# A two-layer decoder trunk on one core: in the attention phases the low halves of the weights, the reciprocals, scalings and copies are emitted some tiles later, and the scores and outputs stand at other tiles

## The chip, the core and the metric

The kernel runs on one core of a Trainium2 chip. The core has a matrix engine (PE, with its weight loads shown as PEld), a vector engine (DVE), a scalar engine (ACT), GpSimd (POOL) and a queue engine that issues the transfers (SP). Each engine runs its own instructions in the order in which the program emitted them and waits for the others by semaphores. The metric is the device time of one execution in microseconds (us); the kernel before takes 544.97 us (median of 3 runs, 544.86 to 545.21).

## The reference, cut to what matters

```
x: 256 tokens x 1024, one sequence; 2 layers; mod = silu(c) @ w_mod[i] + b_mod[i]
layer 0 mixer: causal pooling; layer 1 mixer: attention; after each mixer a squared-ReLU MLP
def moba_attention(h, w_qkv, w_o, rel_bias):      # 16 heads of 64; one block of 256 keys
    q, k, v = split(h @ w_qkv)
    logits = q @ k.T * 64**-0.5 + bias[bucket(distance)]; masked above the diagonal
    o = softmax(logits) @ v
    return o @ w_o
x = x + gate * mixer(modulate(rmsnorm(x)))
x = x + gate * (relu(h @ w_up) ** 2 @ w_down)     # w_up 1024 x 4096, w_down 4096 x 1024
```

All is float32. A block of 256 keys covers the whole sequence, so the choice of blocks drops out.

## The kernel before

Activations lie transposed (128 channels by 256 tokens). Every weight matrix is cut in 128 x 128 tiles, and all tiles of all matrices stand in one stream in the order in which PE uses them; eight tiles are a step. A transfer (`issue`, five 1 MB buffers) brings two steps. For precision each step is split in two: ACT rounds it to a high part `w_hi` (L256), DVE subtracts to get the low part `w_lo` (L266), both three steps ahead of their use. A tile is then two or three matmuls (L278, L279 where the high part meets high and low activations in one 512-column matmul; L284 to L286 otherwise). PE is fed by these streams nearly without a gap; everything else is laid beside them.

The order of all this is written out by hand. `next_columns` is called once for each tile and counts tiles in `now`. `later(d, fn)` puts a piece of work into the program `d` tiles later, `at(t, fn)` puts it at tile `t` of the attention phase. At each multiple of eight it also emits the split of a later step and, at some steps, half of a late modulation vector (`mod_dve`, L308: a product of 128 x 1024 on DVE with a sum along the row). What is emitted earlier stands earlier in its engine's queue; times follow from that and from the waits.

The attention phase counts tiles from 0: tiles 0 to 63 make q and k of head pairs 0 to 3, 64 to 95 the values of these pairs, 96 to 159 q and k of pairs 4 to 7, 160 to 191 their values, 192 to 255 the product with w_o. For each of eight head pairs `p` the class `Pair` emits: `done` (q and k from PSUM to `qk`; for pairs 4 to 7 a copy on ACT, L1021, and an addition on DVE, L1022), `scores` at tile `SCORES_AT[p]` (eight matmuls `sc`, L1031), then with `later` the logits and their row maxima on DVE (L1047, L1053), the exponentials on ACT (L1059), the reciprocals of the sums on DVE (L1064), the scalings on ACT (L1070), the transposes on PE (`pt`, L1076), their copies on ACT (`PT`, L1078), and `outputs` at tile `OUTPUTS_AT[p]` (eight matmuls `po`, L1088 and L1089), split on ACT and DVE into `ol` (L1093, L1096). `qkv_normed` makes the normalised input in eight pieces, with two products on GpSimd (L997, L998) and the two parts on ACT (L494) and DVE (L497).

Of the kernel before, what the change touches and what calls it, by code (L numbers as in the profile page):

```python
# [8 lines left out]
F32 = mybir.dt.float32  # L9
F32R = mybir.dt.float32r  # L10
AF = mybir.ActivationFunctionType
# [4 lines left out]
P = 128  # L16
S = 256
# [62 lines left out]
STEP_QKV = STEP_DN0 + DN_STEPS  # L80
STEP_WO = STEP_QKV + QKV_STEPS
STEP_UP1 = STEP_WO + WO_STEPS
STEP_DN1 = STEP_UP1 + UP_STEPS
# [19 lines left out]
AHEAD = 3  # L103
# [4 lines left out]
N_NORMED, NORMED_AT, NORMED_GAP = 16, 30, 11  # L108

QKV_NORMED_AT, QKV_NORMED_GAP = 29, 6  # L110
SCORES_AT = (46, 65, 84, 103, 122, 138, 155, 172)
OUTPUTS_AT = (108, 116, 125, 145, 203, 208, 213, 218)

# [32 lines left out]
def tile_hybrid_pool_moba(  # L148
# [12 lines left out]
    nc = tc.nc  # L161
# [6 lines left out]
    tmp = ctx.enter_context(tc.tile_pool(name="tmp", bufs=2))  # L168
# [4 lines left out]
    def bank(name):  # L173
        return ps.tile([P, 512], F32, tag="ps", name=name)

    def al_tile(shape, name, dt=F32):
        return act.tile(shape, dt, tag="al", bufs=KF, name=name)
# [74 lines left out]
    def split_hi(h, between=None):  # L252
        raw = loaded["w", h // 2][:, h % 2 * HALF * P : (h % 2 + 1) * HALF * P]
        hi = split_p.tile([P, HALF * P], F32R, tag="whi", name=f"w{h}_hi")
        if between is None:
            nc.scalar.copy(hi, raw)  # L256
        else:
            a = HALF // 2 * P
            nc.scalar.copy(hi[:, :a], raw[:, :a])
            between()  # L260
            nc.scalar.copy(hi[:, a:], raw[:, a:])
        return raw, hi

    def split_lo(h, raw, hi):
        lo = split_p.tile([P, HALF * P], F32R, tag="wlo", name=f"w{h}_lo")
        nc.vector.tensor_sub(lo, raw, hi.bitcast(F32))  # L266
        if h % 2 == 1:
            issue()
        ready.extend((hi, lo, t * P) for t in range(HALF))

    def split(h):
        if h < N_STEPS:
            split_lo(h, *split_hi(h))
# [101 lines left out]
    def modv(layer, m, k=None):  # L375
        assert all((layer, m, j) in known for j in (range(4) if k is None else (k // 2,))), (layer, m)
        return mods[layer, m]
# [115 lines left out]
    def normed_tile(k, u, sh, t, into, high_at, low_at):  # L493
        later(high_at, lambda: nc.scalar.activation(t[:, :S], u, AF.Identity, bias=sh))  # L494

        def low():
            nc.vector.scalar_tensor_tensor(  # L497
                t[:, S:], u, sh, t[:, :S].bitcast(F32), op0=ALU.add, op1=ALU.subtract
            )
            into[k] = t  # L500

        later(low_at, low)
# [98 lines left out]
    for k in range(KD):  # L601
        i, a = divmod(k, KD // 2)
# [73 lines left out]
    class Input:  # L676
# [24 lines left out]
        def all(self, R):  # L701
            self.gain()
            self.scaled(R)
            self.high()
            for k in self.ks:
                self.low(k)
# [5 lines left out]
    def later(d, fn):  # L712
        due.setdefault(now[0] + d, []).append(fn)

    def late_mods(h):
        while late[0] < 2 * len(LATE_STEPS) and LATE_STEPS[late[0] // 2] + late[0] % 2 <= h:
            mod_dve(LATE_MODS[late[0] // 2], late[0] % 2)
            late[0] += 1

    def next_columns():  # L720
        t = now[0]
        todo = due.pop(t, [])
        while todo:
            for fn in todo:
                fn()
            todo = due.pop(t, [])
        if t % HALF == 0:
            h = t // HALF
            if h >= HEAD_STEPS - AHEAD:
                late_mods(h)  # L730
                if STEP_UP1 <= h < STEP_DN1 - AHEAD:

                    w = split_hi(h + AHEAD)
                    later(HALF // 2, lambda: split_lo(h + AHEAD, *w))
                else:
                    split(h + AHEAD)
        now[0] += 1
        return ready.popleft()
# [249 lines left out]
    def at(t, fn):  # L988
        assert t >= now[0] - qkv0, (t, now[0] - qkv0)
        later(t - (now[0] - qkv0), fn)  # L990

    normed = [None] * KD

    def qkv_normed(k):
        t = al_tile([P, 2 * S], f"h10_{k}", F32R)
        u = tmp.tile([P, S], F32, tag="h", bufs=2, name=f"h10_u{k}")
        nc.gpsimd.tensor_scalar_mul(u, xs[k], gs10[:, k : k + 1])  # L997
        nc.gpsimd.tensor_mul(u, u, R[0])  # L998
        normed_tile(k, u, modv(1, 0, k)[:, k : k + 1], t, normed, 6, 10)

    for k in range(KD):
        at(QKV_NORMED_AT + QKV_NORMED_GAP * k, lambda k=k: qkv_normed(k))
# [1 line left out]
    class Pair:  # L1004
        def __init__(self, p):
            self.p = p
            self.qk = None
            self.mx, self.sm, self.rs, self.PT = {}, {}, {}, {}
            at(SCORES_AT[p], self.scores)
            at(OUTPUTS_AT[p], self.outputs)  # L1010

        def done(self, j, b):
            if j == 0:
                self.qk = al_tile([P, 2, S], f"qk{self.p}")
            dst = self.qk[:, j]
            if self.p < NP // 2:
                u, e = unnormed_out(b, R[0], f"qkv{self.p}_{j}")
                later(1, lambda: nc.scalar.activation(dst, u, AF.Identity, bias=e))
            else:
                u = tmp.tile([P, S], F32, tag="u", bufs=5, name=f"qkv{self.p}_{j}_u")  # L1020
                nc.scalar.activation(u, b[:, S:], AF.Copy)  # L1021
                later(2, lambda: nc.vector.tensor_add(dst, b[:, :S], u))  # L1022

        def scores(self):
            p = self.p
            self.sc = [bank(f"sc{p}_{e}") for e in range(2)]
            for t in range(2):
                n = (t + 1) * P
                for e in range(2):
                    rows = slice(e * DH, (e + 1) * DH)  # L1030
                    nc.tensor.matmul(  # L1031
                        self.sc[e][:, t * P : t * P + n], self.qk[rows, 0, t * P : (t + 1) * P],
                        self.qk[rows, 1, :n], start=True, stop=True,
                    )
            self.prob = [al_tile([P, 2, (t + 1) * P], f"L{p}_{t}") for t in range(2)]
            for i, (t, e) in enumerate(((0, 0), (0, 1), (1, 0), (1, 1))):
                later(2 + i, lambda t=t, e=e: self.logits(t, e))
                later(10 + i, lambda t=t, e=e: self.exp(t, e))
                later(16 + i, lambda t=t, e=e: self.normalize(t, e))
            later(34, lambda: self.transposes(0))  # L1040
            later(35, lambda: self.transposes(1))

# [12 lines left out]
        def exp(self, t, e):  # L1055
            L = self.prob[t]
            if e == 0:
                self.sm[t] = tmp.tile([P, 2], F32, tag="sm", bufs=4, name=f"sm{self.p}_{t}")
            nc.scalar.activation(  # L1059
                L[:, e], L[:, e], AF.Exp, bias=self.mx[t][:, e : e + 1], accum_out=self.sm[t][:, e : e + 1]  # L1060
            )
            if e == 1:
                self.rs[t] = tmp.tile([P, 2], F32, tag="rs", bufs=4, name=f"rs{self.p}_{t}")
                nc.vector.reciprocal(self.rs[t], self.sm[t])  # L1064
            if self.p == NP - 1 and t + e == 2:
                nc.scalar.activation(warm, ones, AF.Sqrt)

        def normalize(self, t, e):
            L = self.prob[t][:, e]
# [2 lines left out]
        def transposes(self, e):  # L1072
            p = self.p
            pt = bank(f"pt{p}_{e}")
            for i, src in enumerate((self.prob[0][:, e, :], self.prob[1][:, e, :P], self.prob[1][:, e, P:])):
                nc.tensor.transpose(pt[:, i * P : (i + 1) * P], src, ident)  # L1076
            PT = al_tile([P, 3 * P], f"PT{p}_{e}")
            later(1, lambda: nc.scalar.copy(PT, pt[:, : 3 * P]))  # L1078
            self.PT[e] = PT

        def outputs(self):
            p = self.p
            po = bank(f"po{p}")
            v = values[p // 4]
            for e in range(2):
                a = p % 4 * P + e * DH
                out = slice(e * DH, (e + 1) * DH)
                nc.tensor.matmul(po[out, :S], v[0][:, a : a + DH], self.PT[e][:, :S], start=True, stop=False)  # L1088
                nc.tensor.matmul(po[out, P:S], v[1][:, a : a + DH], self.PT[e][:, S:], start=False, stop=True)  # L1089

            def split_o():
                o = al_tile([P, 2 * S], f"ol{p}", F32R)
                nc.scalar.copy(o[:, :S], po[:, :S])  # L1093

                def low():
                    nc.vector.tensor_sub(o[:, S:], po[:, :S], o[:, :S].bitcast(F32))  # L1096
                    ol[p] = o

                later(1, low)

            later(2, split_o)

    values = [None] * 2

# [26 lines left out]
    for h in range(2):  # L1131
        banks = {}
        for i, (n, k) in enumerate(QKV_ORDER[h * 12 * KD : h * 12 * KD + KD * KD]):
# [4 lines left out]
            if h == 0:  # L1138
                t = raws[k]
# [28 lines left out]
    normed = [None] * KD  # L1168
# [139 lines left out]
```

## Time and profile before

| | |
|---|---|
| median of 3 runs | 544.97 us |
| the profiled execution | 545.22 us, its span 543.4 us |
| mean granted PE clock | 0.994 of full speed |
| PE, PEld, DVE, ACT, POOL busy | 528.6, 475.7, 419.7, 316.8, 17.5 us |
| chain that ended last | PE 78%, DVE 8%, DMA 6%, ACT 4% |
| DVE `w_lo` waits for ACT `w_hi` | 59.4 us in 59 waits |
| transfers | 140.38 MB, 258 GB/s |

The attention phase lies between 232.8 and 352.7 us of the span. The page's busy rows say which engine is full; a timeline of one engine shows each instruction's start, its length, and in square brackets how long the engine stood before it and what ended that wait. Matmuls overlap in it (the next starts before the last has ended), so the pace of PE is read from starts.

### The profile page before, as it was taken

The page shows a single profiled execution, that of the slowest core. Times are in us where ns is not written, and L with a number is a line of the kernel's source. Part 1 is how long each engine was busy: PE and PEld are TensorE (multiplying, and loading weights), DVE is VectorE, ACT ScalarE, POOL GpSimd, SP SyncE. Part 2 cuts the span into 40 slices and gives each one's busy share as a digit, 9 for nine tenths or more (in the row PEclk, how much of TensorE's full clock was granted, in tenths as well). Part 3 has the DMA queues.
Part 4 walks back from the last instruction along what each step waited for, and adds up shares of the span by engine and source line. Part 5 has one row for each costly group of instructions (what it writes and reads, how often), then busy time and mean ns, then how long its engine had stood idle before and what let it go on. Part 6 is the DMA issues. An engine that isn't in the chain of part 4 may idle for free.

```text
span 543.4 us, 10358 instructions
## 1 busy us (share of the span) xinstructions
PE 528.6 (97%) x4108; PEld 475.7 (88%) x4108; DVE 419.7 (77%) x833; ACT 316.8 (58%) x598; POOL 17.5 (3%) x34
## 2 busy tenths in 40 slices
PE   8899999999999999999997999999999999999995
PEld 7767999999988888999776778999998888888895
DVE  2857997899889999857778985888898878765542
ACT  4225336788644545447876886568996645445531
POOL 1000000000000000004500000000000000000000
PEclk9999999999999999999998999999999999999998
DMA  8999998488999999963364686544555675876002
GB/s 330 420 419 415 422 414 311 157 309 307 321 376 397 390 337 356 355 243 117 134 233 154 233 292 224 188 182 175 181 197 193 211 253 194 296 276 241 1 1 77
DMA packets 22336, 140.38 MB, mean 258 GB/s; under 512 B 2416, under 2 KB 4736, under 8 KB 5904
## 3 DMA queue, kind: packets, MB, share of 16 engines
q1 hardware_dynamic: 22048, 138.61, 68.2%
q10 hardware_dynamic: 144, 1.05, 0.5%
q8 instruction: 32, 0.52, 0.4%
q14 instruction: 16, 0.13, 0.1%
q0 software_dynamic: 96, 0.06, 0.0%
HBM read 138.64 MB, written 1.07 MB: 257 GB/s over the span
## 4 chain that ended last, share of the span: by engine, by line
PE 78%; DVE 8%; DMA 6%; ACT 4%; issue 2%; POOL 1%; DVEq 0%; ACTq 0%
PE m1d L278 10%; PE m0d L278 9%; PE m1u L278 5%; PE m0u L284 5%; PE m0u L286 5%; PE m0u L285 5%; PE m0d L279 5%; PE m1d L279 5%; DVE w_lo L266 3%; DMA raw_c_sh<-in_w_mod 3%; PE m1u L284 3%; PE m1u L285 3%; PE m1u L286 3%; PE m1u L279 3%; DMA raw_c_g<-in_w_mod 2%; ACT w_hi L256 2%
## 5 line engine op out<-in xcount | busy, mean ns | idle before, releaser
L266 DVE TENSOR_TENSOR w_lo<-raw_w,w_hi 128x1024 fp32r<-128x1024 f32 x160 | 195.1, 1228 | 60.4 <-ACT w_hi L256 59.4
L256 ACT CAST w_hi<-raw_w 128x1024 fp32r<-128x1024 f32 x159 | 164.7, 1045 | 58.4 <-PE m1d L278 19.7
L278 PE MATMUL m1d<-m1u_al,w_hi 128*128 128x512 f32 x224 | 78.3, 394 | 0.0
L278 PE MATMUL m0d<-m0u_al,w_hi 128*128 128x512 f32 x224 | 78.1, 392 | 0.0
L308 DVE SCALAR_TENSOR_TENSOR raw_m<-raw_m,cact 128x1024 f32<-128x1024 f32 x64 | 77.6, 1217 | 0.0
L284 PE MATMUL m0u<-h,w_hi 128*128 128x256 f32 x248 | 69.8, 281 | 0.0
L286 PE MATMUL m0u<-h,w_lo 128*128 128x256 f32 x248 | 69.6, 281 | 0.1
L285 PE MATMUL m0u<-h,w_hi 128*128 128x256 f32 x248 | 69.4, 280 | 0.0
L279 PE MATMUL m1d<-m1u_al,w_lo 128*128 128x256 f32 x224 | 62.8, 280 | 0.0
L279 PE MATMUL m0d<-m0u_al,w_lo 128*128 128x256 f32 x224 | 62.8, 280 | 0.0
L278 PEld LDWEIGHTS m1d<-m1u_al,w_hi 128*128 128x128 f32 x224 | 42.1, 188 | 9.7
L278 PEld LDWEIGHTS m0d<-m0u_al,w_hi 128*128 128x128 f32 x224 | 42.0, 188 | 9.5
L284 PEld LDWEIGHTS m0u<-h,w_hi 128*128 128x128 f32 x248 | 46.7, 188 | 0.6 <-issue 0.4
L286 PEld LDWEIGHTS m0u<-h,w_lo 128*128 128x128 f32 x248 | 46.7, 188 | 0.3 <-DVE w_lo L266 0.3
L285 PEld LDWEIGHTS m0u<-h,w_hi 128*128 128x128 f32 x248 | 46.7, 188 | 0.0
L278 PE MATMUL m1u<-h,w_hi 128*128 128x512 f32 x128 | 44.4, 394 | 0.0
L279 PEld LDWEIGHTS m1d<-m1u_al,w_lo 128*128 128x128 f32 x224 | 42.1, 188 | 0.0
L279 PEld LDWEIGHTS m0d<-m0u_al,w_lo 128*128 128x128 f32 x224 | 42.1, 188 | 0.0
L284 PE MATMUL m1u<-h_raw,w_hi 128*128 128x258 f32 x128 | 36.5, 285 | 0.0
L285 PE MATMUL m1u<-h_raw,w_hi 128*128 128x256 f32 x128 | 36.3, 284 | 0.0
L286 PE MATMUL m1u<-h_raw,w_lo 128*128 128x258 f32 x128 | 36.2, 283 | 0.0
L279 PE MATMUL m1u<-h,w_lo 128*128 128x256 f32 x128 | 35.5, 277 | 0.0
(207 smaller groups left out, 1047.3 us busy)
## 6 DMA issues: line engine op xcount, KB each, us to landing
raw_w<-in_w_all SPq DMA_DIRECT2D x79, 1024.0 KB, 6.6
raw_m<-in_w_mod SPq DMA_DIRECT2D x32, 1024.0 KB, 6.1
raw_c_sh<-in_w_mod SPq DMA_DIRECT2D x8, 1024.0 KB, 13.9
raw_c_g<-in_w_mod SPq DMA_DIRECT2D x4, 1024.0 KB, 12.6
raw_c_mlp<-in_w_mod SPq DMA_DIRECT2D x2, 1024.0 KB, 11.9
raw_c_shift<-in_w_mod SPq DMA_DIRECT2D x2, 1024.0 KB, 9.1
T<-bd SPq DMA_DIRECT2D x8, 256.0 KB, 7.8
x<-in_xT ACTq DMA_DIRECT2D x1, 1024.0 KB, 5.7
```

Of the source, the lines that this page charges most:

```text
L256: nc.scalar.copy(hi, raw)
L266: nc.vector.tensor_sub(lo, raw, hi.bitcast(F32))
L278: nc.tensor.matmul(b, hi, hl[:, : 2 * S], start=start, stop=False)
L279: nc.tensor.matmul(b[:, S:], lo, hl[:, :S], start=False, stop=stop)
L284: nc.tensor.matmul(dst, hi, xh, start=start, stop=False)
L285: nc.tensor.matmul(dst[:, :S], hi, xl, start=False, stop=False)
L286: nc.tensor.matmul(dst, lo, xh, start=False, stop=stop)
L308: nc.vector.scalar_tensor_tensor(raw[:, a], raw[:, a], 1.0, cact, op0=ALU.mult, op1=ALU.mult, accum_out=dst[:, a : a + 1])
```

## The change

Six things move; no instruction is added or taken away.

- `next_columns`: from the first step of the attention phase on (before: from the second MLP on) `split_lo` of a step, with the `issue` that it holds, comes 4 tiles after `split_hi` and no longer right behind it.
- `exp` 11 instead of 10 tiles after the scores, the reciprocal 5 tiles after its second `exp` (before: at once), `normalize` 22 instead of 16 tiles after the scores.
- `done` of pairs 4 to 7: copy and addition one tile later; copies of the transposes one tile later; `split_o` one tile later.
- `qkv_normed`: three GpSimd buffers of its own instead of two shared ones; high part at 9 instead of 6 tiles, low part at 12 instead of 10.
- `SCORES_AT`: pairs 0, 1 and 4 later by 2, 1 and 2 tiles, pairs 6 and 7 earlier by 3 and 2.
- `OUTPUTS_AT`: 1 to 5 tiles later.

```diff
-SCORES_AT = (46, 65, 84, 103, 122, 138, 155, 172)
-OUTPUTS_AT = (108, 116, 125, 145, 203, 208, 213, 218)
+SCORES_AT = (48, 66, 84, 103, 124, 138, 152, 170)
+OUTPUTS_AT = (112, 121, 130, 147, 205, 210, 214, 219)
@@ next_columns
-                if STEP_UP1 <= h < STEP_DN1 - AHEAD:
+                if STEP_QKV <= h < STEP_DN1 - AHEAD:
                     w = split_hi(h + AHEAD)
                     later(HALF // 2, lambda: split_lo(h + AHEAD, *w))
@@ qkv_normed
-        u = tmp.tile([P, S], F32, tag="h", bufs=2, name=f"h10_u{k}")
+        u = tmp.tile([P, S], F32, tag="hp", bufs=3, name=f"h10_u{k}")
-        normed_tile(k, u, modv(1, 0, k)[:, k : k + 1], t, normed, 6, 10)
+        normed_tile(k, u, modv(1, 0, k)[:, k : k + 1], t, normed, 9, 12)
@@ Pair.done
-                nc.scalar.activation(u, b[:, S:], AF.Copy)
-                later(2, lambda: nc.vector.tensor_add(dst, b[:, :S], u))
+                later(1, lambda: nc.scalar.activation(u, b[:, S:], AF.Copy))
+                later(3, lambda: nc.vector.tensor_add(dst, b[:, :S], u))
@@ Pair.scores
-                later(10 + i, lambda t=t, e=e: self.exp(t, e))
-                later(16 + i, lambda t=t, e=e: self.normalize(t, e))
+                later(11 + i, lambda t=t, e=e: self.exp(t, e))
+                later(22 + i, lambda t=t, e=e: self.normalize(t, e))
@@ Pair.exp
-                nc.vector.reciprocal(self.rs[t], self.sm[t])
+                later(5, lambda: self.reciprocal(t))
@@ Pair.transposes
-            later(1, lambda: nc.scalar.copy(PT, pt[:, : 3 * P]))
+            later(2, lambda: nc.scalar.copy(PT, pt[:, : 3 * P]))
@@ Pair.outputs
-            later(2, split_o)
+            later(3, split_o)
```

On DVE, from the logits of pair 3 to the second half of `qk4`, which the scores of pair 4 need, this stands before (`L` are logits, `mx` row maxima, `raw_m` a modulation vector, `w81_lo` the low half of a step, `ol0` the low part of an output, `rs` a reciprocal); `w80_lo` stands two rows ahead of it:

```order
L1047 SCALAR_TENSOR_TENSOR L3_0_3467<-sc3_1_3462,T3_2056 128x128
L1053 TENSOR_REDUCE mx3_0_3487<-L3_0_3467 128x2
L1022 TENSOR_TENSOR qk4_3472<-qkv4_0_3427,qkv4_0_u_3473 128x256
L1047 SCALAR_TENSOR_TENSOR L3_1_3468<-sc3_0_3461,T3_2056 128x256
L1047 SCALAR_TENSOR_TENSOR L3_1_3468<-sc3_1_3462,T3_2056 128x256
L1053 TENSOR_REDUCE mx3_1_3501<-L3_1_3468 128x2
L1096 TENSOR_TENSOR ol0_3507<-po0_3495,ol0_3507 128x256
L308 SCALAR_TENSOR_TENSOR raw_m_1_4_1_3162,mod1_4_124<-raw_m_1_4_1_3162,cact_107 128x1024
L312 TENSOR_TENSOR mod1_4_124<-mod1_4_124,vec_80 128x2
L266 TENSOR_TENSOR w81_lo_3522<-raw_w_40_3268,w81_hi_3520 128x1024
L1064 RECIPROCAL rs3_0_3534<-sm3_0_3529 128x2
L1022 TENSOR_TENSOR qk4_3472<-qkv4_1_3480,qkv4_1_u_3514 128x256
```

And in the change:

```order
L1047 SCALAR_TENSOR_TENSOR L3_0_3461<-sc3_1_3456,T3_2056 128x128
L1053 TENSOR_REDUCE mx3_0_3482<-L3_0_3461 128x2
L1047 SCALAR_TENSOR_TENSOR L3_1_3462<-sc3_0_3455,T3_2056 128x256
L1022 TENSOR_TENSOR qk4_3468<-qkv4_0_3419,qkv4_0_u_3469 128x256
L1047 SCALAR_TENSOR_TENSOR L3_1_3462<-sc3_1_3456,T3_2056 128x256
L1053 TENSOR_REDUCE mx3_1_3493<-L3_1_3462 128x2
L266 TENSOR_TENSOR w80_lo_3495<-raw_w_40_3285,w80_hi_3471 128x1024
L308 SCALAR_TENSOR_TENSOR raw_m_1_4_1_3180,mod1_4_124<-raw_m_1_4_1_3180,cact_107 128x1024
L312 TENSOR_TENSOR mod1_4_124<-mod1_4_124,vec_80 128x2
L1022 TENSOR_TENSOR qk4_3468<-qkv4_1_3473,qkv4_1_u_3511 128x256
L266 TENSOR_TENSOR w81_lo_3536<-raw_w_40_3285,w81_hi_3516 128x1024
L1099 TENSOR_TENSOR ol0_3529<-po0_3506,ol0_3529 128x256
```

The low half `w80_lo` went behind the logits of pair 3, and `w81_lo`, `ol0` and the reciprocals went behind the second `qk4`.

On PE, before, the scores of pair 6 (`sc6`) stand three tiles into the second half of pair 7:

```order
L278 MATMUL qkv7_1_3777<-h10_1_3066,w83_hi_3630 128x512
L279 MATMUL qkv7_1_3777<-h10_1_3066,w83_lo_3632 128x256
L278 MATMUL qkv7_1_3777<-h10_2_3107,w83_hi_3630 128x512
L279 MATMUL qkv7_1_3777<-h10_2_3107,w83_lo_3632 128x256
L1031 MATMUL sc6_0_3786<-qk6_3664 128x128
L1031 MATMUL sc6_1_3787<-qk6_3664 128x128
```

In the change they stand ahead of that half, at tile 152:

```order
L278 MATMUL qkv7_0_3724<-h10_6_3260,w82_hi_3565 128x512
L279 MATMUL qkv7_0_3724<-h10_6_3260,w82_lo_3594 128x256
L278 MATMUL qkv7_0_3724<-h10_7_3298,w82_hi_3565 128x512
L279 MATMUL qkv7_0_3724<-h10_7_3298,w82_lo_3594 128x256
L1031 MATMUL sc6_0_3764<-qk6_3657 128x128
L1031 MATMUL sc6_1_3765<-qk6_3657 128x128
```

So these scores come three tiles earlier, while the addition that completes `qk6` comes one tile later.

## Rows read from the trace of the kernel before

**Rows 1.** The page: its span and the busy time of each engine.
```profile
span 543.4 us, 10358 instructions
PE 528.6 (97%) x4108; PEld 475.7 (88%) x4108; DVE 419.7 (77%) x833; ACT 316.8 (58%) x598; POOL 17.5 (3%) x34
```
**Rows 2.** Busy time by stretch; columns as its first row names them.
```profile
core 0: us, PE busy (x) PEld busy (x) DVE busy (x) ACT busy (x) POOL busy (x), PEclk, DMA share, GB/s
273.00:324.50 51.50, 48.74 (x285) 37.91 (x284) 44.16 (x94) 39.26 (x106) 0.00 (x0) 0.97 0.63 228
232.80:262.60 29.80, 29.80 (x236) 28.14 (x235) 19.59 (x46) 19.91 (x39) 9.41 (x11) 1.00 0.48 167
...
285.00:295.00 10.00, 7.24 (x40) 5.16 (x39) 7.88 (x20) 6.06 (x18) 0.00 (x0) 0.83 0.57 202
```
**Rows 3.** Timeline of PE, tiles 114 to 126: start, length, instruction, [idle before, releaser].
```profile
282.54 0.40 PE L278 MATMUL qkv<-h,w_hi 128*128 128x512 f32 x1
...
282.89 0.40 PE L278 MATMUL qkv<-h,w_hi 128*128 128x512 f32 x1
...
283.34 0.66 PE L1088 MATMUL po<-PT,v_sb 128*64 128x256 f32 x4
...
284.14 0.50 PE L278 MATMUL qkv<-h,w_hi 128*128 128x512 f32 x1
...
284.60 0.39 PE L278 MATMUL qkv<-h,w_hi 128*128 128x512 f32 x1
...
289.94 0.93 PE L1031 MATMUL sc<-qk 64*128 64x128 f32 x8 [2.76 <-DVE qk L1022]
290.79 0.50 PE L278 MATMUL qkv<-h,w_hi 128*128 128x512 f32 x1
...
294.82 0.39 PE L278 MATMUL qkv<-h,w_hi 128*128 128x512 f32 x1
```
**Rows 4.** Timeline of PE, three other places where it stands.
```profile
272.00 0.73 PE L1117 MATMUL v<-w_hi,h 128*128 128x512 f32 x2 [0.55 <-DVE h L497]
...
279.04 0.65 PE L1088 MATMUL po<-PT,v_sb 128*64 128x256 f32 x2
...
280.35 0.50 PE L278 MATMUL qkv<-h,w_hi 128*128 128x512 f32 x1
...
326.85 0.38 PE L284 MATMUL wo<-ol,w_hi 128*128 128x256 f32 x1 [0.73 <-ACT PT L1078]
```
**Rows 5.** Timeline of PE, the scores of pairs 6 and 7.
```profile
307.73 0.93 PE L1031 MATMUL sc<-qk 64*128 64x128 f32 x8
...
315.32 0.93 PE L1031 MATMUL sc<-qk 64*128 64x128 f32 x8
```
**Rows 6.** Timeline of DVE, tiles 88 to 163.
```profile
273.05 1.22 DVE L308 SCALAR_TENSOR_TENSOR raw_m<-raw_m,cact 128x1024 f32<-128x1024 f32 x1
...
278.56 1.23 DVE L266 TENSOR_TENSOR w_lo<-raw_w,w_hi 128x1024 fp32r<-128x1024 f32 x1 [0.69 <-ACT w_hi L256]
...
282.88 1.22 DVE L266 TENSOR_TENSOR w_lo<-raw_w,w_hi 128x1024 fp32r<-128x1024 f32 x1 [1.90 <-ACT w_hi L256]
...
289.48 0.40 DVE L1022 TENSOR_TENSOR qk<-qkv,qkv_u 128x256 f32<-128x256 f32 x1
...
292.29 1.23 DVE L266 TENSOR_TENSOR w_lo<-raw_w,w_hi 128x1024 fp32r<-128x1024 f32 x1 [2.01 <-ACT w_hi L256]
...
305.48 0.42 DVE L1022 TENSOR_TENSOR qk<-qkv,qkv_u 128x256 f32<-128x256 f32 x1
...
308.13 1.22 DVE L266 TENSOR_TENSOR w_lo<-raw_w,w_hi 128x1024 fp32r<-128x1024 f32 x1 [0.46 <-ACT w_hi L256]
...
314.32 0.42 DVE L1022 TENSOR_TENSOR qk<-qkv,qkv_u 128x256 f32<-128x256 f32 x1
```
**Rows 7.** Timelines of POOL and DVE where a GpSimd product meets a `w_lo`.
```profile
258.44 0.73 POOL L998 TENSOR_TENSOR h_u<-h_u,n_R 128x256 f32<-128x256 f32 x1
...
258.62 1.62 DVE L266 TENSOR_TENSOR w_lo<-raw_w,w_hi 128x1024 fp32r<-128x1024 f32 x1
```

More of the change, by code (lines that the diff above doesn't have):

```diff
@@ L1062, in exp, with reciprocal @@
             if e == 1:
-                self.rs[t] = tmp.tile([P, 2], F32, tag="rs", bufs=4, name=f"rs{self.p}_{t}")
-                nc.vector.reciprocal(self.rs[t], self.sm[t])
+                later(5, lambda: self.reciprocal(t))
             if self.p == NP - 1 and t + e == 2:
                 nc.scalar.activation(warm, ones, AF.Sqrt)
+        def reciprocal(self, t):
+            self.rs[t] = tmp.tile([P, 2], F32, tag="rs", bufs=4, name=f"rs{self.p}_{t}")
+            nc.vector.reciprocal(self.rs[t], self.sm[t])
         def normalize(self, t, e):
```

## The prediction

> **What bounds the kernel now.** I read the page first. PE counts as busy for 528.6 of 543.4 us [rows 1], so nearly all that can be won at once is time in which PE stands, or runs slowly. Next, the busy time by stretch: outside the attention phase PE is full, and in it one stretch of 10 us sticks out, with PE busy for 7.24 us and its granted clock at a mean of 0.83 [rows 2]. Then the timeline of PE there: it stands for 2.76 us before the scores of pair 4, until DVE has done `qk` [rows 3]. Then the timeline of DVE, to see why: that addition stands in the program at tile 114, which PE began at 282.54 [rows 3], but DVE began it at 289.48 [rows 6], 6.9 us late. DVE's queue runs in order, and in front of the addition two `w_lo` stood still for 0.69 and 1.90 us, until ACT had rounded `w_hi` [rows 6]; what was queued behind them and ready, logits and sums, waited with them. So the phase is bound by PE, with a vector queue that lags and at four places comes too late.
>
> **What the lag costs now.** By place:
> - values of pairs 0 to 3, the last low part from DVE: 0.55 us [rows 4];
> - outputs of pair 0: 279.04 to 280.35, 1.31 us, where the same outputs of pair 1 took 283.34 to 284.14, 0.80 us: 0.51 us [rows 3, 4];
> - scores of pair 4: 2.76 us [rows 3];
> - the half clock after it. From 290.79 to 294.82 PE did four tiles and one set of outputs in 4.03 us. At full clock a tile is 282.54 to 282.89, 0.35, and two tiles with outputs are 282.89 to 284.60, 1.71 [rows 3], so 1.71 + 2 x 0.35 = 2.41. The excess is 1.62; I take 1.5, since the tile behind a set of outputs is 0.1 longer anyway (284.14 to 284.60);
> - a bank of the product with w_o, held until ACT has copied a transpose: 0.73 us [rows 4].
>
> Sum 0.55 + 0.51 + 2.76 + 1.5 + 0.73 = 6.05 us. This is all that the change can give back that I can price; it adds no work to PE.
>
> **The change part by part.** No instruction is added or removed, so the durations stay and only waits can change.
>
> *Low halves half a step later.* DVE now meets `w_lo` after the logits that are ready and gives ACT four tiles (1.4 us) more to round. That alone covers the waits of 0.69, 1.90 (most of it) and 0.46 us [rows 6]. What it may cost: a low half is emitted 20 and not 24 tiles ahead of its use, 7.0 and not 8.4 us, and DVE's lag now was 6.9. If the lag stayed, PE would run into the low halves; since the lag was made by these waits, I price this at 0, at most one stall of 0.5 us. The transfer issued with each odd low half goes 1.4 us later too; SP waits there for DVE to free the buffer, and transfers fill 0.63 of the stretch [rows 2], so 0 again.
>
> *Is DVE early enough for the scores?* I add up DVE's work between fixed points in the old trace, without its waits, and move it to the new order. First the latest case, in which DVE begins the vector of tile 88 no earlier than now, at 273.05 [rows 6].
> - To the second `qk4`: 289.48 - 273.05 = 16.43, less 0.69 and 1.90 of waits, is 13.84; `w81_lo` (1.23, as the row at 292.29) now stands behind it: 12.6. It begins at 285.65 and is done by 286.05. PE was ready for these scores at 289.94 - 2.76 = 287.18; two tiles later is +0.70, the first two stalls are gone, -1.06: 286.8. It holds, by 0.75 us.
> - To the second `qk6`: 305.48 - 289.48 = 16.0, less 2.01, is 13.99; one low half for another, one `ol` more (0.4): 14.4. Done by 300.45. PE: from the scores of pair 4 to those of pair 6, 307.73 - 289.94 = 17.79 [rows 3, 5], less 1.5 of clock, less 5 tiles (33 become 28, -1.75): 14.54, so 301.3. It holds, by 0.85.
> - To the second `qk7`: 314.32 - 305.48 = 8.84, less 0.46, is 8.38: done by 308.85. PE: 315.32 - 307.73 = 7.59 [rows 5] and one tile more, 0.35: 309.25. It holds, by 0.4.
>
> These margins are thin, but they are the worst ones: DVE should reach tile 88 earlier than 273.05, since the low halves in front of it waited too. As a whole, DVE has 44.16 us of work in the 51.50 us from 273.0 to 324.5, ACT 39.26 [rows 2]; PE without its stalls there needs 51.50 - 0.51 - 2.76 - 1.5 = 46.7. DVE is then full to 95% and can keep up only if it nearly never waits. So I leave 0.4 us of new small stalls in the sum.
>
> *Reciprocals, scalings, copies later.* They take DVE and ACT off results that are not there yet. Nothing waits for them early: the transposes stay 34 tiles behind the scores, the last scaling is 25 behind. Cost 0; the bound is the 0.73 of the w_o bank, if the copies of pair 6 come late again. They are emitted at tiles 188 and 189 (before 190 and 191) and stand ahead of the scalings of pair 7, so I count this 0.73 as won.
>
> *Scores of pairs 0, 1 and 4 later.* Their transposes go with them, and the outputs of pairs 0 and 1 that read these move by 4 and 5 tiles, more than the scores: nothing gets tighter, 0. *Scores of pairs 6 and 7 earlier.* In the sum above. *Outputs later.* The outputs of pairs 4 to 7 end 6 tiles ahead of their use now, and 3 or 4 tiles after the change, 1.1 to 1.4 us plus the 0.9 of the next outputs; the two parts take about 0.4 each on ACT and DVE (the `qk` rows, [rows 6]). Price 0, bound 0.5 each.
>
> *Third GpSimd buffer.* It lets GpSimd run ahead, so ACT and DVE find the normalised pieces ready; it should remove the 0.55 of the values. While a GpSimd product of 0.73 us ran, a `w_lo` took 1.62 us in place of 1.23 [rows 7, 6]. GpSimd's 16 products now fall earlier, into a stretch in which DVE is busy for 19.59 of 29.80 us [rows 2], which hides them. The Trainium skill's "SBUF — State Buffer" (section "SBUF: two separate sides") has it that a VectorE instruction with two SBUF inputs and a GpSimd one hold a shared port in turn, one fully blocking the other; the longer row agrees. By that rule the third buffer may make such clashes more frequent, and each (1.62 - 1.23 = 0.39 us) would eat most of the thin margin at pair 7: the sum would be up to 0.4 us higher.
>
> **The sum.** The profiled execution took 545.22 us (span 543.4 and 1.8 around it). 545.22 - 6.05 + 0.4 = 539.57. It stands 0.25 above the median of the runs, 544.97: 539.3 us.
>
> **The rivals.**
> - *A wait comes back at one of the scores* (DVE 95% full): DVE misses the margin at pair 6 or 7 by 1 to 3 us, and a stall as long as the old one halves the clock again. That returns 1 us (no clock loss) to 2.76 + 1.5 = 4.3 us: 540.3 to 543.6. For it: the load of DVE; against it: the sums above hold even with a late start.
> - *The change doesn't do what it says*: DVE lags from its load and not from the order, and the waits only change place: 544 to 546. Against it: 5.06 us of DVE standing idle between 273 and 315 [rows 6], beside work that was ready.
> - *Slower: the scores of pair 6 are too early.* Addition at tile 147, scores at 152: 5 tiles and one set of outputs, 5 x 0.35 + 1.0 = 2.75 us; before it was 9 tiles and the outputs, 4.15. If DVE is there as late as it was at tile 114, 6.9 us, PE stands 6.9 + 0.4 - 2.75 = 4.5 us and loses 1.5 by the clock; at pair 7 (7 tiles, 2.45 us) and the outputs behind it 1.3 more. That is 7.3 against the 6.05 won: 546.2 us. It loses from a lag of about 5.7 us on. Against it: with such a lag DVE would not have stood idle.
>
> **How the numbers follow.** What a measurement of this kernel can tell from no change is about 0.2%, 1.1 us. Forecast 0.60 (its own range 538.4 to 540.4), wait back at a score 0.22, no change in effect 0.07, slower 0.11. Faster is the first two: 0.82; same 0.07; slower 0.11. The range takes the forecast's and nearly all of the first rival: 538.2 to 543.8. The low end is the whole 6.05 and 0.5 of small waits that I did not price.
>
> **What would show it.** Right: no wait of PE over 0.5 us before the scores of pair 4, 6 and 7; granted clock 1.00 through the attention phase; the `w_lo` rows of DVE without the 1.9 and 2.0 us waits; the first matmul of the second MLP about 6 us earlier; everything behind it unchanged in length. Wrong: PE waiting for `qk` at pair 6 or 7, for a `w_lo` or for `ol`, or a stretch with the clock under 0.9. If DVE's idle time in the phase is as large as now, the order was not the cause.

## The result and the profile after

The changed kernel takes 539.05 us (median of 4 runs, 538.82 to 539.27), the kernel before 544.91 us beside it (4 runs, 544.71 to 545.21): a ratio of 0.9892, 95% interval 0.9875 to 0.9909. The profiled execution took 539.27 us. The forecast was 539.3. That it came so close is in part luck: the attention phase won 0.64 us more than the sum said, 0.68 us were lost behind it where the sum had nothing, and 0.4 us of small stalls, which the sum had, did not come. These errors nearly cancel.

The page after, the two rows that answer to [rows 1] (the engines' counts are those of before; the eight instructions more are semaphore events, which are not counted as work):

```profile
span 537.5 us, 10366 instructions
PE 526.3 (98%) x4108; PEld 474.6 (88%) x4108; DVE 420.1 (78%) x833; ACT 316.2 (59%) x598; POOL 18.9 (4%) x34
```

Busy time by stretch, columns and stretches as in [rows 2]:

```profile
232.80:262.60 29.80, 29.80 (x237) 28.13 (x236) 20.64 (x46) 19.06 (x36) 13.83 (x14) 1.00 0.49 172
...
273.00:324.50 51.50, 51.50 (x331) 41.45 (x329) 47.31 (x99) 44.16 (x113) 0.00 (x0) 1.00 0.67 241
285.00:295.00 10.00, 10.00 (x71) 7.50 (x68) 9.38 (x23) 7.20 (x22) 0.00 (x0) 1.00 0.67 236
```

PE is full and at full clock in the stretch in which it had stood and run at half clock (7.24 of 10 us, clock 0.83, [rows 2]). The timeline of PE after, at the places of [rows 3 to 5] and at the border to the second MLP:

```profile
279.58 0.66 PE L1091 MATMUL po<-PT,v_sb 128*64 128x256 f32 x4
...
280.39 0.50 PE L278 MATMUL qkv<-h,w_hi 128*128 128x512 f32 x1
...
286.44 0.93 PE L1031 MATMUL sc<-qk 64*128 64x128 f32 x8
...
300.95 0.93 PE L1031 MATMUL sc<-qk 64*128 64x128 f32 x8
...
308.91 0.93 PE L1031 MATMUL sc<-qk 64*128 64x128 f32 x8
...
346.15 0.28 PE L284 MATMUL m1u<-h_raw,w_hi 128*128 128x258 f32 x1
...
352.38 0.39 PE L286 MATMUL m1u<-h_raw,w_lo 128*128 128x258 f32 x1
...
352.97 0.50 PE L403 MATMUL n_rms<-ones,n_acc 128*128 128x1 f32 x4
353.71 0.61 PE L403 MATMUL n_rms<-ones,n_sq 128*128 128x1 f32 x4 [0.24 <-ACT n_sq L392]
```

No matmul of the phase has a wait in brackets any more; the outputs of pair 0 take 0.81 us (279.58 to 280.39), as those of pair 1 did. Of the kernel before, the same border:

```profile
352.84 0.28 PE L284 MATMUL m1u<-h_raw,w_hi 128*128 128x258 f32 x1
...
359.72 0.58 PE L403 MATMUL n_rms<-ones,n_sq 128*128 128x1 f32 x4
```

So the attention phase won 352.84 - 346.15 = 6.69 us, and 0.68 of it was lost again at once: from the first `m1u` to the second sums of the norm (`n_sq`) it is 6.88 us before and 7.56 after. What follows is as long as it was, to 0.1 us. On DVE the waits of [rows 6] are gone:

```profile
271.49 1.21 DVE L308 SCALAR_TENSOR_TENSOR raw_m<-raw_m,cact 128x1024 f32<-128x1024 f32 x1
...
281.12 1.22 DVE L266 TENSOR_TENSOR w_lo<-raw_w,w_hi 128x1024 fp32r<-128x1024 f32 x1
...
283.59 0.42 DVE L1022 TENSOR_TENSOR qk<-qkv,qkv_u 128x256 f32<-128x256 f32 x1
...
298.50 0.42 DVE L1022 TENSOR_TENSOR qk<-qkv,qkv_u 128x256 f32<-128x256 f32 x1
...
307.55 0.42 DVE L1022 TENSOR_TENSOR qk<-qkv,qkv_u 128x256 f32<-128x256 f32 x1
```

The additions for pairs 4, 6 and 7 (the three `qk` rows) are done at 284.01, 298.92 and 307.97, and PE begins their scores 2.43, 2.03 and 0.94 us later.

### The profile page after: what moved, and what is told of

It is laid out like the page before. It is cut to its first block, busy times and chain, and to the rows that moved or that the text cites. A ratio compares the mean times of both kernels' runs of the same rounds, so it can differ in the third digit from the quotient of the medians.

```text
span 537.5 us, 10366 instructions
## 1 busy us (share of the span) xinstructions
PE 526.3 (98%) x4108; PEld 474.6 (88%) x4108; DVE 420.1 (78%) x833; ACT 316.2 (59%) x598; POOL 18.9 (4%) x34
## 4 chain that ended last, share of the span: by engine, by line
PE 88%; DMA 6%; DVE 3%; ACT 1%; issue 0%; DVEq 0%; ACTq 0%
PE m1d L278 10%; PE m0d L278 10%; PE m0u L284 6%; PE m1u L278 6%; PE m0u L286 5%; PE m0u L285 5%; PE m1d L279 5%; PE m0d L279 5%; PE v L1120 4%; PE qkv L278 3%; DMA raw_c_sh<-in_w_mod 3%; PE m1u L279 3%; PE m1u L284 2%; PE m1u L285 2%; PE m1u L286 2%; DMA raw_c_g<-in_w_mod 2%
```

## The experiments

Eleven kernels. The kernel before was timed beside each of the three groups: 544.81, 544.86 and 544.74 us. All numbers are medians; the ratio is to the kernel before.

**Low halves alone.** The kernel before with

```
-                if STEP_UP1 <= h < STEP_DN1 - AHEAD:
+                if STEP_QKV <= h < STEP_DN1 - AHEAD:
```

> The kernel before with one edit alone: in the attention phase the low half of a step comes four tiles after its rounding; scores, outputs, delays and buffers stay as before. Theory (the two low halves that waited for ACT made the vector queue late): the waits of 0.69 and 1.90 us go, the second qk4 is done by about 286 instead of 289.9, PE is ready for the scores of pair 4 no earlier than 286.1, so that stall of 2.76 us and the half clock behind it (1.5) are gone; the 0.55 at the values, the 0.51 at the outputs and the 0.73 at the w_o bank may stay. 544.9 less 4.3, plus the 0.6 us that the changed kernel lost behind the phase: about 541.2, range 540.0 to 542.0. Rival (it is the tiles of scores and outputs that count): the stall before the scores of pair 4 stays above 2 us, 544 to 545.

538.90 us (538.60 to 539.03), ratio 0.9891 (0.9877 to 0.9904): all of the change's gain from one of its six parts. Its PE, the scores of pair 4, and the only wait in brackets that is left:

```profile
285.59 0.93 PE L1031 MATMUL sc<-qk 64*128 64x128 f32 x8
...
353.55 0.60 PE L403 MATMUL n_rms<-ones,n_sq 128*128 128x1 f32 x4 [0.24 <-ACT n_sq L392]
```

I had expected 541.2, since I had given the stops at the values, at the outputs of pair 0 and at the w_o bank to other parts of the change. They went with the low halves too. The rival falls. The edit also moves the transfer that is issued with a low half; that it has no part in the gain was not tested by itself, but the softmax delays (below) win nearly as much and leave it where it was.

**All but the low halves.** The changed kernel with that line undone.

> The changed kernel with the low halves put back right behind their rounding; everything else of the change stays. Theory: the vector queue waits again for ACT (waits of 1 us and more at w_lo between 270 and 310), the addition of qk4 is late by some 5 to 7 us again; the scores of pair 4 stand two tiles later than before, so PE stands 1 to 2.1 us there, loses 1 to 1.5 us by the clock, and stands again at pair 6, whose scores are earlier: 541.5 to 544.5; behind the phase the 0.6 us lost at the second norm are not lost. Rival (scores and outputs, not the low halves): no stall over 0.5 us, 538.4 to 539.1.

542.02 us, ratio 0.9948 (0.9934 to 0.9961): the time fits, the place does not. DVE has no wait for a low half between 272 and 303 and pair 4 has no stop. PE stands earlier, at transposes and values, and at pair 7:

```profile
266.86 0.44 PE L1079 MATMUL pt<-vec,L 128*128 128x128 f32 x2 [0.36 <-ACT L L1073]
...
311.83 0.93 PE L1031 MATMUL sc<-qk 64*128 64x128 f32 x8 [0.65 <-DVE qk L1022]
```

and in its list of waits (engine, line, waited for: total us, times, longest) ACT waits six times for reciprocals that now come five tiles later:

```profile
ACT L L1073 <- DVE rs L1069: 6.0, 6, 1.4
```

So the other parts also end the lag, in another way, and cost something themselves when the low halves are not moved; the delays alone (below) narrow down which of them.

**Tables alone.** The kernel before with the new `SCORES_AT` and `OUTPUTS_AT`.

> The kernel before with the new tiles of scores and outputs alone. Theory (low halves make the queue late): the scores of pair 4 are two tiles later, so their stall falls from 2.76 to about 2.1 us, the half clock stays, and the scores of pair 6, three tiles earlier, now come before their addition and stand 1 to 3 us: 544 to 547. Rival (the tiles are what counts): the stall at pair 4 goes, 539 to 541.

545.55 us (544.11 to 546.14), ratio 1.0005 (0.9995 to 1.0014). The time is that of the kernel before. The stop before pair 4 is shorter, and the next one stands at pair 5, not at pair 6 as I had written:

```profile
289.70 0.93 PE L1031 MATMUL sc<-qk 64*128 64x128 f32 x8 [1.53 <-DVE qk L1022]
...
298.93 1.59 PE L1031 MATMUL sc<-qk 64*128 64x128 f32 x8 [1.88 <-DVE qk L1022]
```

**Normalised input alone.** The kernel before with the three GpSimd buffers and the parts at 9 and 12 tiles.

> The kernel before with the part on the normalised input alone: three GpSimd buffers of their own, high part at 9 and low part at 12 tiles. Theory: the 0.55 us at the values go; DVE reaches tile 88 up to 0.5 us earlier, but still waits for ACT at the two low halves, so the scores of pair 4 stall 2.2 to 2.8 us: 544.0 to 544.7. Rival (the late start of the queue at tile 88 is what makes it late): the stall at pair 4 falls by 1 us or more and with it the half clock, 541 to 543. Against both: if the products on GpSimd lengthen vector work by more than they free, 545.0 to 545.5.

543.26 us, ratio 0.9974 (0.9964 to 0.9984). The stop at the values is gone and the one at pair 4 is nearly as long as before, as the theory had it. In the profiled execution the clock stayed up behind that stop, and PE then stood 1.21 us at pair 5, where it had not stood before. Its PE, and two stretches of it (PE, PEld, DVE, ACT, POOL busy, clock, DMA share, GB/s):

```profile
289.37 0.93 PE L1031 MATMUL sc<-qk 64*128 64x128 f32 x8 [2.68 <-DVE qk L1022]
...
298.60 0.93 PE L1031 MATMUL sc<-qk 64*128 64x128 f32 x8 [1.21 <-DVE rs L1064]
```
```profile
13.00:18.00 5.00, 5.00 (x47) 4.53 (x40) 3.57 (x18) 1.45 (x4) 0.00 (x0) 0.50 1.01 411
...
291.00:293.00 2.00, 2.00 (x16) 1.37 (x15) 1.29 (x2) 1.76 (x4) 0.00 (x0) 1.00 1.00 320
```

From the first matmul of the phase to the first of the second MLP this execution took 352.09 - 233.65 = 118.44 us, for 352.84 - 232.79 = 120.05 before. But it is the slowest of its eight (544.26, as I had expected): it ran at half clock near the start (the first row) and came to the phase 0.86 us late. Why the others are below what I had expected was not profiled.

**The low half that came back.** In the changed kernel the low half of step 98 now stands directly ahead of the last residual sum on DVE, and PE's first `w_lo` matmul of that step began 0.05 us after the low half was done (352.38, shown above):

```profile
351.11 1.22 DVE L266 TENSOR_TENSOR w_lo<-raw_w,w_hi 128x1024 fp32r<-128x1024 f32 x1
352.24 0.48 DVE L490 SCALAR_TENSOR_TENSOR x<-wo,mod,x 128x256 f32<-128x256 f32 x1
```

The changed kernel with that step left out:

```
-                if STEP_QKV <= h < STEP_DN1 - AHEAD:
+                if STEP_QKV <= h < STEP_UP1 - 1 or STEP_UP1 <= h < STEP_DN1 - AHEAD:
```

> The changed kernel, but the low half of the last step that is split before the second MLP (step 98) comes right behind its rounding again; all others stay four tiles later. In the changed kernel this low half stood ahead of the last residual sum on the vector queue, ended at 352.33, PE waited for it (352.07 to 352.38 where 0.12 is usual) and then 0.38 us for the squares of that sum. Theory (this one low half is the cause of what came back behind the phase): both waits go, the first matmul of the second MLP stays at about 346.1, all behind it 0.5 to 0.7 us earlier: 538.4 us, 538.2 to 538.7. Rival (the chain of sums behind the product with w_o is too long at the faster pace, whatever stands in it): the wait before the squares stays at 0.3 us or more: 538.8 to 539.1.

538.35 us (538.15 to 538.61), ratio 0.9878 (0.9865 to 0.9891). The low half now fills a gap of DVE, the last sum comes 1.2 us earlier, and both waits of PE are gone (352.50 to 352.87 is 0.37, where it was 0.36 before and 0.74 in the changed kernel):

```profile
349.11 1.22 DVE L266 TENSOR_TENSOR w_lo<-raw_w,w_hi 128x1024 fp32r<-128x1024 f32 x1
...
351.04 0.48 DVE L490 SCALAR_TENSOR_TENSOR x<-wo,mod,x 128x256 f32<-128x256 f32 x1
```
```profile
352.50 0.50 PE L403 MATMUL n_rms<-ones,n_acc 128*128 128x1 f32 x4
352.87 0.58 PE L403 MATMUL n_rms<-ones,n_sq 128*128 128x1 f32 x4
```

**The best short version.** That condition put into the kernel before, and nothing else.

> The kernel before with the low halves four tiles later from the first attention step on, save that of step 98; nothing else of the change. By the run with the low halves alone (538.9, no wait of PE in the phase) less the 0.5 to 0.6 us of the low half of step 98: 538.3 us, 538.0 to 538.6. Rival (the other parts of the change are needed to fill what is won): 538.8 or more.

538.33 us (538.06 to 538.54), ratio 0.9877 (0.9865 to 0.9890), as fast as the one above: one line beats both kernels (the changed kernel's fastest run is 538.82), and the other five parts add nothing that can be measured to it.

**Delays alone.** The kernel before with all that is emitted later, but for the low halves and the normalised input.

> The kernel before with the delays alone (exponentials, reciprocals, scalings, copies, additions, splits of the outputs some tiles later); low halves, tables and GpSimd buffers as before. All of the change but the low halves gave 542.0 with no wait of a low half between 272 and 303. Theory (the delays do that: ACT no longer stands in front of a rounding on a reciprocal that DVE has not reached): those waits shrink below 0.7 us, the stall before the scores of pair 4 falls under 0.5: 541.0 to 543.0. Rival (it was the tiles of the scores that took pair 4 out of the stall): the waits of 1.9 and 2.0 stay, the stall at pair 4 is above 1.5 us: 543.5 to 545.5.

539.73 us, ratio 0.9904 (0.9891 to 0.9917), better than expected: a second way to the same end that moves no low half. PE stands only 0.47 us at the values and 0.48 at pair 4. All but the low halves (542.02) is this kernel with the tables and the normalised input, and nothing else: so it is these two that cost 2.3 us there, alone or together.

**Pair 4 later.** `SCORES_AT[4]` from 122 to 130 in the kernel before.

> The kernel before with one number changed: the scores of pair 4 at tile 130 instead of 122 (their transposes go with them). Eight tiles are 2.8 us, about the stall. Theory 1 (the lag of DVE does harm only where PE asks for it): no stall at pair 4, a gain of 2.9 us and of the half clock: 540.3 to 542.0. Theory 2 (the lag stays in the queue and the next one that asks pays): PE stands 1 to 2 us at pair 5 (tile 138) or a low half: 543.0 to 544.5.

545.18 us (543.63 to 545.91), ratio 0.9997 (0.9985 to 1.0008): no gain, and more than theory 2 had said, though it is theory 2 that the trace shows, at a place that I had not named. The scores of pair 4 have no wait any more; the outputs of pair 2 pay, three tiles behind the old place, since ACT has not copied their transposes:

```profile
290.33 0.65 PE L1088 MATMUL po<-PT,v_sb 128*64 128x256 f32 x2 [2.20 <-ACT PT L1078]
```

Why ACT was late there stands in its own timeline and DVE's (the same rows stand in the kernel before, 0.1 us later); the copy (L1078) is the next instruction behind the scaling:

```profile
289.51 0.40 ACT L1070 ACTIVATE L<-L,rs 128x128 f32<-128x128 f32 x1 [1.53 <-DVE rs L1064]
```
```profile
288.18 1.23 DVE L266 TENSOR_TENSOR w_lo<-raw_w,w_hi 128x1024 fp32r<-128x1024 f32 x1
289.32 0.16 DVE L1064 RECIPROCAL rs<-sm 128x2 f32<-128x2 f32 x1
```

ACT stood 1.53 us at a scaling, for a reciprocal that DVE had queued behind a low half. And the next low half waits in turn for a rounding that ACT has queued behind that scaling: 2.01 us at 292.20 here, as at 292.29 in [rows 6]. So two queues that run in order wait for each other by turns: this is the ring of which the next runs speak.

**Which delays break the ring.** First the three of the softmax alone (exponentials 11, reciprocal 5 later, scalings 22), then the others alone (copies, additions, copies of the transposes, splits).

> The kernel before with three delays alone: exponentials one tile later, the reciprocal five tiles after its exponential, the scalings 22 instead of 16 tiles after the scores. All the delays together gave 539.7. Theory (two queues that wait for each other: in the kernel before ACT stands 1.54 us at a scaling for a reciprocal that is queued on DVE behind a low half, which waits for a rounding that is queued on ACT behind such scalings): these three break the ring, the waits of 1.9 and 2.0 us at the low halves go, no stall over 0.7 us at pair 4: 539.5 to 540.5. Rival (it is the copies, additions and splits being later that keep ACT free): the stall at pair 4 stays above 1.5 us: 543.5 to 545.5.

539.46 us, ratio 0.9901 (0.9887 to 0.9914). DVE waits for no low half between 272 and 299; the stop at pair 4 is what is left:

```profile
287.09 0.93 PE L1031 MATMUL sc<-qk 64*128 64x128 f32 x8 [0.47 <-DVE qk L1022]
```

> The kernel before with the other delays alone: copies and additions of pairs 4 to 7, copies of the transposes and splits of the outputs one tile later. Theory (ring between reciprocal, scaling, rounding and low half): nothing is broken, the low halves wait 1.5 to 2 us as before, and the addition that the scores of pair 4 need comes one tile later, so their stall is as long as before: 544.3 to 545.5. Rival: the stall goes with these: 539.5 to 541.

544.91 us, ratio 1.0003 (0.9993 to 1.0013): nothing is won. Pair 4 stands, and the w_o bank stands for longer than the 0.73 of [rows 4]:

```profile
289.45 1.65 PE L1031 MATMUL sc<-qk 64*128 64x128 f32 x8 [2.49 <-DVE qk L1022]
...
326.69 0.39 PE L284 MATMUL wo<-ol,w_hi 128*128 128x256 f32 x1 [1.15 <-ACT PT L1081]
```

The ring theory holds on both sides: the ring is broken by moving the low half on DVE, or by moving the softmax pieces (which of the three does it was not separated), and not by moving what lies outside it.

**Scores 6 and 7 still earlier.** The changed kernel with 148 and 167.

> The changed kernel with the scores of pair 6 at tile 148 instead of 152 (the first tile at which their addition stands ahead of them) and those of pair 7 at 167 instead of 170. In the changed kernel the addition for pair 6 was done at 298.92 and its scores began at 300.95; for pair 7 307.97 and 308.91. Four tiles are 1.4 us, three are 1.0. By these margins (2.03 and 0.94): no stall at pair 6, at most 0.2 us at pair 7, time as the changed kernel, 538.9 to 539.3. By the worst case of the prediction (margins of 0.85 and 0.4): stalls of 0.55 and 0.65 us, 540.0 to 540.5; more, with the half clock behind them, if the lag of DVE is what it was.

539.53 us, ratio 0.9903 (0.9889 to 0.9916), between the two times that I had given. Pair 6 has no wait, so the margin of 2.03 us was real. Pair 7 stands 0.47 us in brackets, since its addition waits for ACT's copy:

```profile
308.00 0.93 PE L1031 MATMUL sc<-qk 64*128 64x128 f32 x8 [0.47 <-DVE qk L1022]
```
```profile
307.52 0.42 DVE L1022 TENSOR_TENSOR qk<-qkv,qkv_u 128x256 f32<-128x256 f32 x1 [0.81 <-ACT qkv_u L1021]
```

## Why the prediction was right, and where not

- *The bound.* Right: the lag of DVE behind its waits for `w_hi` was what PE paid for. Shown by the low halves alone (538.90) and, from the other side, by the scores of pair 4 moved away from the stop (545.18: the next to ask paid). What I had not seen is that the lag was kept up by a ring of both queues; I had priced the later reciprocals and scalings at 0, and together with the later exponentials they win 544.74 - 539.46 = 5.3 us alone. This gain is not on top of that of the low halves: each ends the same lag.
- *The sum of 6.05 us* was too small: the phase won 6.69. The first matmul of the product with w_o came 324.54 - 318.84 = 5.70 us earlier (terms: 5.32), the rest behind it 0.99 (term: 0.73). The terms were mis-sized because I took the wait in brackets for the loss. A bracket begins at the modelled end of the last matmul, but at full pace the next one starts before that end: a matmul of 512 columns lasts 0.40 us and the next starts after 0.23. In the kernel before:

```profile
270.37 0.40 PE L1117 MATMUL v<-w_lo,h 128*128 128x512 f32 x1
270.60 0.62 PE L1117 MATMUL v<-w_hi,h 128*128 128x512 f32 x2
271.06 0.40 PE L1117 MATMUL v<-w_lo,h 128*128 128x512 f32 x1
...
276.03 0.28 PE L279 MATMUL qkv<-h,w_lo 128*128 128x256 f32 x1
276.24 0.93 PE L1031 MATMUL sc<-qk 64*128 64x128 f32 x8
...
286.89 0.28 PE L279 MATMUL qkv<-h,w_lo 128*128 128x256 f32 x1
...
325.84 0.28 PE L286 MATMUL wo<-ol,w_lo 128*128 128x256 f32 x1
...
327.07 0.28 PE L285 MATMUL wo<-ol,w_hi 128*128 128x256 f32 x1
```

  From 271.06 to the matmul at 272.00 [rows 4] is 0.94, less the usual 0.23 is 0.71, where the bracket says 0.55. At the scores of pair 4 it is 289.94 - 286.89 = 3.05, less the usual 0.21 (276.03 to 276.24) is 2.84, where the bracket says 2.76. With the half clock as measured (1.62, taken as 1.5) this makes 0.36 of the missing 0.38 (more on this term in the last section). At the w_o bank it is 326.85 - 325.84 = 1.01, less the usual 0.12 is 0.89, and the matmul behind the stop lasts 0.10 longer than usual (326.85 to 327.07): 0.99, all of it.
- *0.4 us of new small stalls in the phase*: there were none. DVE reached tile 88 at 271.49, 1.56 us earlier than the worst case that I had reckoned with, and the margins were 2.43, 2.03 and 0.94 us instead of 0.75, 0.85 and 0.4.
- *Everything behind unchanged in length*: wrong, and the step that failed is the price of the low halves, 0, at most one stall of 0.5 us. I looked for it in the attention phase, where DVE and ACT have the lag, and not at the last step, where the later low half passes the residual sum that the next norm waits for. It cost 0.68 us; putting this one back wins 539.05 - 538.35 = 0.70.
- *Third buffer, 0.55 at the values; copies earlier than the scalings, 0.73 at the w_o bank.* The buffers with their later parts do take the first away (normalised input alone), but they are not needed for it: with the low halves alone both stops are gone. The later copies, with the additions and splits, made the second longer, 1.15 us: that step failed, the 0.73 was won by the end of the lag.
- *The port.* GpSimd was busy 13.83 us in the first stretch where it was 9.41 [rows 2], and its products lengthened more of DVE's instructions, as I had weighed. The mean `h` (L497) became 552 ns from 477, the longest beside this product:

```profile
251.19 1.14 POOL L998 TENSOR_TENSOR h_u<-h_u,n_R 128x256 f32<-128x256 f32 x1
```
```profile
251.66 0.95 DVE L497 SCALAR_TENSOR_TENSOR h<-h_u,mod,h 128x256 fp32r<-128x256 f32 x1
```

  DVE's 46 instructions of that stretch took 20.64 us for 19.59, and PE waited for none of it. The Trainium skill's "SBUF — State Buffer" (section "SBUF: two separate sides") lets the two engines hold a shared port in turn; the longer rows agree, but the up to 0.4 us that the sum would have had more by that rule did not arise.
- *The rivals.* No wait came back at a score. That the lag comes from the load falls with the low halves alone. Scores of pair 6 too early: four tiles (1.4 us) earlier still they have no wait, and the addition is done 0.63 us ahead of them (298.39 and 299.02 in that run).

## What to carry to other kernels

When two engines with queues in order hand work to each other in both directions, a wait of one at the wrong place in its queue returns as a wait of the other some instructions later; look for such a ring first, and break it at the cheapest of its links, because moving the instruction that pays only moves the bill. When emission is shifted in a whole stretch, follow the shifted instruction into the last step and see what it now stands ahead of. And take the loss of a pipelined engine from start to start, less the usual distance, not from the idle time that the trace prints.

## What was not expected of the hardware

The half clock behind a stop does not follow from the stop's length. After 2.76 us (the kernel before, [rows 3]) the granted clock fell to a mean of 0.53 from 291 to 294; after 2.68 us with the normalised input alone it stayed at 1.00; with the tables alone it stayed at 1.00 behind 1.53 us and fell to 0.51 behind 1.88:

```profile
291.00:293.00 2.00, 2.00 (x14) 1.57 (x14) 0.95 (x1) 2.00 (x6) 0.00 (x0) 1.00 0.97 369
...
299.00:301.00 2.00, 2.00 (x11) 1.35 (x12) 1.97 (x6) 2.00 (x6) 0.00 (x0) 0.51 1.00 389
```

The executions of two kernels with such a stop fall in two groups: pair 4 later, 543.63 to 544.18 (five) and 545.14 to 545.91 (seven); tables alone, 544.11 to 544.63 (five) and 545.55 to 546.14 (six). Kernels without a stop in the phase spread over 0.4 to 0.5 us. The mean granted clock of each execution parts the groups without overlap: 0.996 to 0.998 against 0.990 to 0.993, and 0.998 to 0.999 against 0.990 to 0.996. Both profiles are of the upper group and have the half clock. For tables alone a mean of 0.998 leaves at most 0.0025 x 544 = 1.4 us of lost clock in the whole execution, less than the 1.7 us that the profiled one lost in the phase, so its lower group did not have that half clock.

For the kernel before the same sign says that the term of 1.5 us does not stand by itself. Of its 50 executions beside the experiments 13 have a mean of 0.998, so they did not lose the 1.7 us of [rows 2] either (0.17 of 10 us). Their median is 544.56, only 0.3 us under that of the 26 at 0.993 to 0.995 (544.84). So an execution without the half clock was not 1.5 us faster: most of it must have been paid in another way. A stop at the next scores, as with the normalised input alone, is the likely one, but none of these executions was profiled.
